# A trunk layer's first modulation: shifts from column groups of the PE array, input scaling and low parts on DVE

## Chip, cores and metric

One core of one Trainium2 chip runs the whole layer. The metric is the device time of one execution in microseconds; three executions of the kernel before took 1581.88, 1586.55 and 1586.59 us (median 1586.55).

## What is computed

A hybrid trunk layer on 1024 latent and 256 context tokens with 1024 features: RMS norm and modulation, a wide input projection, two recurrent mixers (mLSTM and HGRN2), an output projection, a second norm and modulation, a convolutional feed-forward part and a last norm. The part that this document is about is its beginning:

```python
mod_l = (jax.nn.silu(c) @ w_mod[l] + b_mod[l])[:, None, :]
mod_c = (jax.nn.silu(c_ctx) @ w_mod[l] + b_mod[l])[None, None, :]
sh1, sc1, g1, sh2, sc2, g2 = jnp.split(mod_l, N_MOD, axis=-1)
sh1c, sc1c, g1c, sh2c, sc2c, g2c = jnp.split(mod_c, N_MOD, axis=-1)
pl = _modulate(_rmsnorm(xl, norm1_w[l]), sh1, sc1) @ w_in[l]
pc = _modulate(_rmsnorm(xc, norm1_w[l]), sh1c, sc1c) @ w_in[l]
# _modulate(h, shift, scale) = h * (1 + scale) + shift
```

## The kernel before, in words

Everything is float32. A matmul on the fast path takes a pair: `hh` is x rounded to the matmul's format, `hl` the remainder, and the weights likewise `wh` and `wl`; the product is hh·wh + hh·wl + hl·wh. Features lie on the partitions, in eight blocks of 128 (k = 0 to 7), tokens along the free dimension.

**Loading and norm.** SP's queue loads small tensors, then the eight blocks of x (L197), then, in the order of the string `LOADS`, shift weights (`sh_load`, L236), scale weights (`sc_load`, L244) and value weights (`w_load`). ACT squares the blocks, DVE sums them, TensorE adds over the partitions (`row_rstd`, L216), POOL takes the power -1/2, and `row_bc` (L226) spreads the result over all partitions into `rbc`, in two halves.

**First modulation.** j = 0 is the conditioning vector c (latent tokens), j = 1 is c_ctx (context). The scale columns come from DVE dot products with an accumulator: `mod_scale(k, j)` (L260) multiplies block k of the transposed weights with silu(c), broadcast over the partitions in `scb[j]`, and sums along the row. The shift columns come in two ways: for k in `MPE` = (1, 5) from eight matmuls with two moving columns (`mod_shift_mm`, L248; each float32 matmul is two instructions in the trace), for the other six k from a second DVE dot product inside `mod_scale`, once for j = 0 and once for j = 1.

**h.** For k = 0 (`DN`), DVE's `h_scale` (L279) forms x·rbc·a in one operation, ACT adds the shift and rounds (`h_hi`), and DVE forms the remainder (`h_lo`). For the others POOL multiplies x by rbc (`h_norm`, L275), ACT forms hh with scale and shift and then the unrounded value over x (two operations, L288 and L289), and DVE subtracts (L299).

**Rounds.** The value projection of the mLSTM goes in three rounds of token groups: LAT0 (the loop at L400; five token tiles in five PSUM banks, 3 x 5 matmuls a step), LAT1 (L437, three tiles) and CTX (L471, two tiles), with the gate matmuls (L459) between. `split` casts half a weight tile on ACT (`wh`) and subtracts on DVE or POOL (`wl`), two halves a call. In the loop of LAT0 the split of every second k goes to POOL (L405). In the loop of LAT1 the scales and shifts of j = 1 are formed (`mod_scale(order[k], 1)`, L447), and after steps 4 and 7 four context blocks each go through POOL (norm), ACT and DVE (`h_ctx`, L431). From L454 and L476 on, DVE also does the first dot products of the second modulation (`mod2_tile`).

**Order.** In this whole part the order of the instructions on ACT, SP, DVE, POOL and TensorE is the order in the source (`manual_schedule`, L80 and L175); every engine works its queue in that order. After L492 ACT and TensorE keep a hand-written order and a planner orders DVE, POOL and SP. Small PSUM tiles (`sc_tile`) rotate over three banks.

Of the kernel before, what the change touches and what calls it, by code (L numbers as in the profile page):

```python
# [35 lines left out]
QF = (0, 1, 2)  # L36
MPE = (1, 5)
DN = (0,)
MODR = (2, 4, 5, 6, 6, 6, 6, 6, 6)
# [38 lines left out]
def kernel(ctx: ExitStack, tc: tile.TileContext, A: dict, out: bass.AP):  # L78
# [102 lines left out]
    SY.dma_start(out=crow, in_=A["crow"])  # L181
    scc = sp.tile([P, 16], F32, name="scc")
    S.activation(scc, cc, AF.Silu)
    scb = [vp.tile([P, D], F32, name="scl"), sp.tile([P, D], F32, name="scb")]
# [46 lines left out]

    sccv = scc.rearrange("p (j k) -> p k j", k=KD)
    modw = {}
    modc = [(sp2.tile([P, 2], F32, name="sh", bufs=8), sp2.tile([P, 2], F32, name="a1", bufs=8)) for _ in range(KD)]

    def sh_load(k):  # L236
        if k in MPE:
            modw["h", k] = sp2.tile([P, KD, P], F32, name="wsh", tag="ld", bufs=8)
            SY.dma_start(out=modw["h", k], in_=A["wsh"][k].rearrange("p (a c) -> p a c", a=KD))
        else:  # L240
            modw["h", k] = sp2.tile([P, D], F32, name="wsh", tag="ld", bufs=8)
            SY.dma_start(out=modw["h", k], in_=A["wsc"][k * P:(k + 1) * P, :])

# [3 lines left out]

    def mod_shift_mm(k):  # L248
        modw["m", k] = sc_tile("md")
        for kk in range(KD):  # L250
            PE.matmul(modw["m", k][:, 0:2], modw["h", k][:, kk, :], sccv[:, kk, :], start=(kk == 0), stop=(kk == KD - 1))

    def mod_shift_out(k):
        V.tensor_scalar(modc[k][0], modw["m", k][:, 0:2], bmod[:, k:k + 1], None, op0=ALU.add)

    def mod_dot(w, j, dst):
        junk = w if j else stage("junk", 2)
        V.scalar_tensor_tensor(junk, w, 1.0, scb[j], op0=ALU.mult, op1=ALU.mult, accum_out=dst)

    def mod_scale(k, j):  # L260
        aj = modc[k][1][:, j:j + 1]
        mod_dot(modw["c", k], j, aj)
        if k not in MPE:
            hj = modc[k][0][:, j:j + 1]
            mod_dot(modw["h", k], j, hj)
            V.tensor_scalar(hj, hj, bmod[:, k:k + 1], None, op0=ALU.add)
        V.tensor_scalar(aj, aj, b1[:, k:k + 1], n1w[:, k:k + 1], op0=ALU.add, op1=ALU.mult)
# [14 lines left out]
    def h_hi(k, j):  # L282
        x_, hi = h_cols(k, j)
        sh, a1 = modc[k]
        if j == 0 and k in DN:
            S.activation(hi, x_, AF.Identity, bias=sh[:, 0:1])
            return
        S.activation(hi, x_, AF.Identity, bias=sh[:, j:j + 1], scale=a1[:, j:j + 1])  # L288
        S.activation(x_, x_, AF.Identity, bias=sh[:, j:j + 1], scale=a1[:, j:j + 1])  # L289

    def h_lo(k, j):
# [3 lines left out]
        lo = hl[k][:, 0:TC] if j else hl[k][:, TC:TA]  # L295
        if j == 0 and k in DN:
            V.scalar_tensor_tensor(lo, x_, modc[k][0][:, 0:1], raw(hi), op0=ALU.add, op1=ALU.subtract)
        else:
            V.tensor_tensor(lo, x_, raw(hi), op=ALU.subtract)  # L299
# [34 lines left out]

    def v_mm(po, toks, k, wh, wl, mid=None, ks=(0, KD - 1)):
        for x, w, first, last in ((hh, wh, True, False), (hh, wl, False, False), (hl, wh, False, True)):
            if last and mid is not None:
                mid()
            for t in toks:
                PE.matmul(po[t], x[k][:, t * P:(t + 1) * P], w, start=(k == ks[0] and first), stop=(k == ks[1] and last))  # L340
# [30 lines left out]
    load("w", 2)  # L371
    mod_scale(0, 0)
    wgr = sp.tile([P, KD, 16], F32, name="wgr")
    wgt = sp.tile([P, KD, 32], F32R, name="wgt")
    rbc = stage("rbc", 1)
    row_bc(rrs[0], 4, rbc[:, x7g[0]])
    h_scale(0, rbc, x7g[0])
    row_bc(rrs[1], 4, rbc[:, x7g[1]])
    h_scale(0, rbc, x7g[1])
    if 1 in MPE:  # L380
        mod_shift_mm(1)
    h_hi(0, 0)
    for k in range(1, 1 + NA):
        if k not in DN:
            h_norm(k, rbc, 0, G)
    mod_scale(1, 0)
    split(V)
    load("w", 3)
    SY.dma_start(out=wgr, in_=A["wgt"].rearrange("p (a c) -> p a c", a=KD))
    if 1 in MPE:  # L390
        mod_shift_out(1)
    h_lo(0, 0)
    if 1 in DN:
        h_scale(1, rbc, slice(0, T))
    h_hi(1, 0)
# [4 lines left out]
    for k in range(KD):  # L400
        v_mm(po, LAT0, k, *wq[k], mid=(lambda: mod_shift_mm(2)) if k == 0 and 2 in MPE else None)
        if k + 3 in MPE:
            mod_shift_mm(k + 3)
        if k % 2 == 0:
            split(G)  # L405
        if k + 2 < KD:
            if k + 2 in MPE:
                mod_shift_out(k + 2)
            mod_scale(k + 2, 0)
        if k + 1 < KD:  # L410
            h_lo(k + 1, 0)
        if k + 2 < KD:
            h_hi(k + 2, 0)
        if k in (2, 4, 6):
            load("w", k // 2 - 1)
        if k + 1 + NA < KD:
            h_norm(k + 1 + NA, rbc, 0, G)
        if k == KD - 2:
# [1302 lines left out]
```

## Time and profile before

| what | value |
|---|---|
| median of three runs | 1586.55 us |
| profiled execution | 1585.19 us |
| its span, first to last instruction | 1583.4 us |
| mean granted TensorE clock | 0.977 |
| TensorE busy (matmuls) | 1504.9 us, 95% |
| DVE / ACT / POOL busy | 1136.1 / 551.2 / 639.1 us |
| first hgrn value matmul (L547) | 127.92 us |

The page of the profile gives shares over the whole span; TensorE is busy in 95% of it, and the chain of work that ended last lies on TensorE for 71%. The first tenth of the span looks different from the rest, so the rows below are taken from there: the stretches are cut at the round's first and last matmuls and at the moments at which the granted clock changed. PEclk is the share of full speed that was granted: 1.00 is 2.4 GHz and 0.50 is 1.2 GHz.

### The profile page before, as it was taken

The numbers are of one execution on the slowest core, as the hardware profiler recorded it, in microseconds if no ns is written. First come the engines' busy times: TensorE is split into PE (matmuls) and PEld (weight loads), VectorE is DVE, ScalarE is ACT, GpSimd is POOL, SyncE is SP. The second block draws the span as 40 slices with busy tenths as digits, with TensorE's granted clock in tenths as the row PEclk, the third lists the DMA queues.
The fourth block names the chain that finished last, engine by engine and source line by source line (L and its number), as shares of the span: only waits on it lengthen the run. The fifth ranks groups of instructions, "written<-read, shape, count | busy, mean of one in ns | idle before, by whom it ended". The sixth has DMA issues, their size and how long they took to land.

```text
span 1583.4 us, 22327 instructions
## 1 busy us (share of the span) xinstructions
PE 1504.9 (95%) x8822; PEld 1226.3 (77%) x8822; DVE 1136.1 (72%) x1474; ACT 551.2 (35%) x948; POOL 639.1 (40%) x525
## 2 busy tenths in 40 slices
PE   7889999999899999998999999999999998998998
PEld 4667788888777787877867888888888886886886
DVE  6996666879567776767487989889898898226334
ACT  4543242443232442434463322222222223224332
POOL 3665234453335645443322433333333335335341
PEclk7899999999999999999999999999999999999999
DMA  9235541212032111024667111111111114111112
GB/s 368 88 121 158 171 121 40 67 57 72 32 108 70 42 55 42 30 74 140 218 205 284 54 41 54 53 41 53 52 42 54 43 38 159 54 54 41 43 38 106
DMA packets 47790, 141.76 MB, mean 90 GB/s; under 512 B 4803, under 2 KB 14915, under 8 KB 47686
## 3 DMA queue, kind: packets, MB, share of 16 engines
q1 hardware_dynamic: 47686, 140.34, 26.1%
q8 instruction: 69, 1.13, 0.3%
q14 instruction: 35, 0.29, 0.1%
HBM read 119.81 MB, written 12.13 MB: 83 GB/s over the span
## 4 chain that ended last, share of the span: by engine, by line
PE 71%; DVE 7%; POOL 2%; issue 2%; ACT 2%; DMA 1%; POOLq 0%; SPq 0%; ACTq 0%; DVEq 0%
PE pu L1432 29%; PE pd L1578 14%; PE po L1288 3%; PE pl_hg L512 3%; PE pl_zb L512 3%; PE pl_zf L512 3%; PE pl_mo L512 2%; PE pl_mq L512 2%; PE pc L512 1%; PE pl_hq L512 1%; PE ap L1091 1%; DVE G L1493 1%; POOL QQ L1128 1%; PE st L879 1%; PE pl_mk L512 1%
## 5 line engine op out<-in xcount | busy, mean ns | idle before, releaser
L1432 PE MATMUL pu<-low,wh 128*128 128x512 f32 x1216 | 374.5, 389 | 0.0
L135 ACT CAST wh<-wst 128x512 fp32r<-128x512 f32 x184 | 112.0, 620 | 529.6 <-issue 227.5
L137 POOL TENSOR_TENSOR wl<-wst,wh 128x512 fp32r<-128x512 f32 x114 | 150.7, 1324 | 355.8 <-ACT wh L135 342.7
L1432 PEld LDWEIGHTS pu<-low,wh 128*128 128x128 f32 x1216 | 228.3, 188 | 47.4
L1432 PE MATMUL pu<-low,wl 128*128 128x512 f32 x608 | 236.5, 389 | 0.0
L1493 DVE SCALAR_TENSOR_TENSOR G<-pu,fcw,G 128x945 f32<-128x945 f32 (+2 forms) x168 | 205.3, 1222 | 23.9 <-ACT G L1486 19.0
L1493 DVE SCALAR_TENSOR_TENSOR cb<-pu,fcw,cb 128x945 f32<-128x945 f32 (+2 forms) x168 | 205.3, 1222 | 23.7 <-ACT cb L1486 17.6
L1578 PE MATMUL pd<-wh,gd 128*128 128x512 f32 x624 | 196.7, 397 | 11.7 <-DVE gd L1526 6.9
L1526 DVE TENSOR_TENSOR gd<-G,gd 128x1024 fp32r<-128x1024 f32 x41 | 57.1, 1393 | 131.2 <-ACT gd L1525 131.0
L1578 PEld LDWEIGHTS pd<-wh,gd 128*128 128x128 f32 x624 | 119.6, 192 | 38.3 <-DVE gd L1526 8.0
L1128 POOL TENSOR_TENSOR QQ<-QQ,FF 128x256 f32<-128x256 f32 x112 | 108.1, 987 | 81.5 <-PE ap L1091 41.3
L1432 PEld LDWEIGHTS pu<-low,wl 128*128 128x128 f32 x608 | 114.2, 188 | 23.6
L1578 PE MATMUL pd<-wl,gd 128*128 128x512 f32 x312 | 123.6, 396 | 0.0
L1524 POOL TENSOR_TENSOR wl<-wst,wh 128x512 fp32r<-128x512 f32 x40 | 73.5, 1840 | 115.1 <-ACT wh L1523 115.0
L137 DVE TENSOR_TENSOR wl<-wst,wh 128x512 fp32r<-128x512 f32 x70 | 57.7, 844 | 56.6 <-ACT wh L135 56.4
L1525 ACT CAST gd<-G 128x1024 fp32r<-128x1024 f32 x43 | 45.0, 1049 | 132.8 <-PE pd L1578 126.1
L1578 PEld LDWEIGHTS pd<-wl,gd 128*128 128x128 f32 x312 | 59.8, 192 | 12.7
L331 POOL TENSOR_TENSOR wl<-wst,wh 128x512 fp32r<-128x512 f32 x26 | 50.0, 1943 | 46.3 <-ACT wh L329 26.4
L1121 DVE TENSOR_TENSOR KK<-KK,FF 128x768 f32<-128x768 f32 (+1 forms) x56 | 52.1, 941 | 15.9 <-PE tps L1107 12.5
L1555 POOL TENSOR_TENSOR G<-G,cb 128x1024 f32<-128x1024 f32 x22 | 53.9, 2451 | 14.9 <-DVE cb L1493 14.9
L877 POOL TENSOR_SCALAR kw<-ktok,WS 128x128 f32<-128x128 f32 x60 | 23.9, 399 | 53.7 <-PE st L879 53.5
L1084 ACT COPY X<-KK 128x512 f32<-128x512 f32 x40 | 26.9, 682 | 46.6 <-DVE KK L1121 33.6
(395 smaller groups left out, 3147.7 us busy)
## 6 DMA issues: line engine op xcount, KB each, us to landing
wst<-in_wup_dram SPq DMA_DIRECT2D x44, 512.0 KB, 3.2
wst<-in_wcm_dram SPq DMA_DIRECT2D x28, 512.0 KB, 3.3
wst<-in_wmod_dram SPq DMA_DIRECT2D x26, 512.0 KB, 3.4
wst<-in_wout_dram SPq DMA_DIRECT2D x24, 512.0 KB, 3.5
wst<-in_wdown_dram SPq DMA_DIRECT2D x22, 512.0 KB, 3.2
wst<-in_wvml_dram SPq DMA_DIRECT2D x10, 512.0 KB, 3.5
x<-in_xcT_dram SPq DMA_DIRECT2D x8, 512.0 KB, 6.5
wsc<-in_wsc_dram SPq DMA_DIRECT2D x8, 512.0 KB, 8.8
```

What stands on the lines that cost most here:

```text
L135: S.copy(wh, st[:, hs_])
L137: (eng or G).tensor_tensor(wl, st[:, hs_], raw(wh), op=ALU.subtract)
L331: eng.tensor_tensor(wl, si, raw(wh), op=ALU.subtract)
L512: PE.matmul(o, w[:, ws], x[k][:, c0:c1], start=(k == 0 and pi == 0), stop=(k == KD - 1 and pi == 2))
L1121: V.tensor_tensor(kv, kv, tk, op=ALU.mult)
L1128: G.tensor_tensor(qv, qv, tq, op=ALU.mult)
L1432: PE.matmul(pl[:, gs], w[:, ws], x[k][:, gs], start=(k == 0 and pi == 0), stop=(k == KD - 1 and pi == 2))
L1493: V.scalar_tensor_tensor(a3[:, r0:r1, c0:c1], s3[:, r0 + dy:r1 + dy, c0 + dx:c1 + dx], wcol((dy + 1) * 3 + dx + 1), a3[:, r0:r1, c0:c1], o ...
L1524: G.tensor_tensor(wl, src, raw(wh), op=ALU.subtract)
L1526: (G if dh == 0 and c < 3 else V).tensor_tensor(gl, Gt[c], raw(gh), op=ALU.subtract)
L1555: G.tensor_tensor(Gt[j], Gt[j], cb, op=ALU.mult)
L1578: PE.matmul(po[t], x[:, ts_], w, start=(c == 0 and pi == 0), stop=(c == NF - 1 and pi == 2))
```

## The change

All shift columns come from TensorE now, for both j at once. The silu of both vectors is written into two of 32 zeroed columns per block (`sccp`), so that a block is a 128x32 stationary operand; the shift weights, 128 columns a block and now loaded in the layout of `wsh` for every k, are the moving one. `mod_mm` sends blocks kk and kk + 4 to the column group of 32 that kk names, so four partial sums lie on four groups of 32 partitions; `mod_copy` brings them to SBUF on ACT, `mod_flip` sums and transposes them with a matmul against two selection columns (`sel`, loaded from the start of `lmask0`), and `mod_out` adds the bias on DVE. `mod_scale` keeps its scale dot product only. Every k takes the way of k = 0: `h_scale` on DVE, one ACT operation, and `h_lo` with the shift added. The splits inside the loop of LAT0 go to DVE. `h_norm` on POOL stays for the context blocks only.

```diff
-    scc = sp.tile([P, 16], F32, name="scc")
-    S.activation(scc, cc, AF.Silu)
+    sel = sp.tile([P, 2], F32, name="sel")
+    SY.dma_start(out=sel, in_=A["lmask0"][:, 0:2])
+    sccp = sp.tile([P, KD, 32], F32, name="sccp")
+    V.memset(sccp, 0.0)
+    S.activation(sccp[:, :, 0:2], cc.rearrange("p (j k) -> p k j", k=KD), AF.Silu)
...
-    def mod_shift_mm(k):
-        modw["m", k] = sc_tile("md")
+    def mod_mm(k):
+        modw["p", k] = md = sc_tile("md")
         for kk in range(KD):
-            PE.matmul(modw["m", k][:, 0:2], modw["h", k][:, kk, :], sccv[:, kk, :], start=(kk == 0), stop=(kk == KD - 1))
...
+            j = slice(32 * (kk % 4), 32 * (kk % 4) + 32)
+            PE.matmul(md[j, 0:P], sccp[:, kk, :], modw["h", k][:, kk, :], start=(kk < 4), stop=(kk >= 4))
+
+    def mod_copy(k):
+        modw["s", k] = sp2.tile([P, TC], F32, name="mds", tag="sqc")[:, 0:P]
+        S.copy(modw["s", k], modw["p", k][:, 0:P])
+
+    def mod_flip(k):
+        PE.matmul(modw["p", k][:, P:P + 2], modw["s", k], sel, start=True, stop=True)
+
+    def mod_out(k):
+        V.tensor_scalar(modc[k][0], modw["p", k][:, P:P + 2], bmod[:, k:k + 1], None, op0=ALU.add)
...
-        mod_dot(modw["c", k], j, aj)
-        if k not in MPE:
-            hj = modc[k][0][:, j:j + 1]
-            mod_dot(modw["h", k], j, hj)
-            V.tensor_scalar(hj, hj, bmod[:, k:k + 1], None, op0=ALU.add)
+        w = modw["c", k]
+        V.scalar_tensor_tensor(w if j else stage("junk", 2), w, 1.0, scb[j], op0=ALU.mult, op1=ALU.mult, accum_out=aj)
...
-    mod_scale(0, 0)
...
+    mod_mm(0)
+    mod_copy(0)
     row_bc(rrs[0], 4, rbc[:, x7g[0]])
+    mod_scale(0, 0)
+    mod_flip(0)
+    mod_out(0)
     h_scale(0, rbc, x7g[0])
     row_bc(rrs[1], 4, rbc[:, x7g[1]])
+    mod_mm(1)
+    mod_copy(1)
     h_scale(0, rbc, x7g[1])
-    if 1 in MPE:
-        mod_shift_mm(1)
-    h_hi(0, 0)
-    for k in range(1, 1 + NA):
-        if k not in DN:
-            h_norm(k, rbc, 0, G)
-    mod_scale(1, 0)
+    mod_flip(1)
     split(V)
...
+    h_hi(0, 0)
+    mod_out(1)
     h_lo(0, 0)
-    if 1 in DN:
-        h_scale(1, rbc, slice(0, T))
+    mod_scale(1, 0)
+    h_scale(1, rbc, slice(0, T))
     h_hi(1, 0)
...
     for k in range(KD):
-        v_mm(po, LAT0, k, *wq[k], mid=(lambda: mod_shift_mm(2)) if k == 0 and 2 in MPE else None)
-        if k + 3 in MPE:
-            mod_shift_mm(k + 3)
-        if k % 2 == 0:
-            split(G)
-        if k + 2 < KD:
-            if k + 2 in MPE:
-                mod_shift_out(k + 2)
-            mod_scale(k + 2, 0)
+        n = k + 2
+        v_mm(po, LAT0, k, *wq[k], mid=((lambda: mod_mm(n), lambda: mod_copy(n)), (lambda: mod_flip(n),)) if n < KD else ())
         if k + 1 < KD:
             h_lo(k + 1, 0)
-        if k + 2 < KD:
-            h_hi(k + 2, 0)
+        if n < KD:
+            mod_scale(n, 0)
+            mod_out(n)
+            h_scale(n, rbc, slice(0, T))
+            h_hi(n, 0)
+        if k % 2 == 0:
+            split(V)
         if k in (2, 4, 6):
             load("w", k // 2 - 1)
-        if k + 1 + NA < KD:
-            h_norm(k + 1 + NA, rbc, 0, G)
```

`v_mm` takes two lists of calls as `mid`, one run after its first set of five matmuls and one after its second.

## Rows read from the trace of the kernel before

**Rows 1.** Stretches: us, busy us (and instructions) of each engine, PEclk, DMA share, GB/s.

```profile
17.43:29.45 12.02, 9.61 (x49) 9.15 (x49) 9.31 (x15) 2.88 (x5) 7.69 (x4) 0.56 1.03 420
29.45:39.35 9.90, 8.03 (x18) 5.83 (x19) 9.79 (x14) 4.69 (x6) 5.42 (x4) 0.50 0.96 353
39.35:49.60 10.25, 5.64 (x25) 4.35 (x25) 10.18 (x9) 4.91 (x6) 8.82 (x4) 1.00 0.57 194
49.60:59.80 10.20, 10.20 (x34) 8.66 (x33) 10.09 (x12) 4.13 (x5) 10.20 (x4) 0.50 0.17 51
59.80:75.87 16.07, 15.11 (x64) 11.49 (x62) 13.88 (x18) 9.86 (x14) 7.56 (x5) 1.00 0.10 33
75.87:106.45 30.58, 26.68 (x114) 19.10 (x114) 28.25 (x47) 13.43 (x27) 23.75 (x20) 0.94 0.36 125
106.45:127.92 21.47, 17.06 (x76) 12.71 (x74) 15.48 (x26) 10.16 (x19) 12.23 (x8) 0.84 0.38 127
```

**Rows 2.** Timeline of PE: start, us, instructions, [idle before <-releaser]; waits, round ends.

```profile
36.12 2.33 PE L340 MATMUL pv<-wh,hl 128*128 128x512 f32 x5
...
49.24 2.19 PE L340 MATMUL pv<-wh,hl 128*128 128x512 f32 x5 [4.61 <-DVE hl L299]
...
74.58 1.29 PE L340 MATMUL pv<-wh,hl 128*128 128x512 f32 x5
...
86.70 0.49 PE L229 MATMUL rb<-cst,rr 128*128 128x128 f32 x2 [2.01 <-POOL rr L223]
...
114.95 1.22 PE L340 MATMUL pv<-wh,hh 128*128 128x512 f32 x2 [2.88 <-ACT wh L329]
...
124.60 0.28 PE L463 MATMUL gpc<-hh,wgt 128*32 128x256 f32 x1
...
127.92 0.49 PE L547 MATMUL pv<-wh,hh 128*128 128x512 f32 x1
```

**Rows 3.** Timeline of DVE, one operation beside POOL and one alone.

```profile
42.60 3.30 DVE L258 SCALAR_TENSOR_TENSOR junk<-wsh,scl 128x1024 f32<-128x1024 f32 x1
...
61.32 1.21 DVE L258 SCALAR_TENSOR_TENSOR junk<-wsc,scl 128x1024 f32<-128x1024 f32 x1
```

**Rows 4.** Timeline of SP's queue, the issue ahead of the x loads.

```profile
1.18 0.33 SPq L181 DMA_DIRECT2D crow<-in_crow_dram  x1
```

**Rows 5.** Timeline of PE: row broadcast; later column-grouped matmuls between 512-wide pairs.

```profile
19.84 4.27 PE L229 MATMUL rb<-cst,rr 128*128 128x128 f32 x16 [0.16 <-POOL rr L223]
...
459.65 0.62 PE L512 MATMUL pl_hq<-hh,wl 128*128 128x512 f32 x2
460.21 0.46 PE L1091 MATMUL ap<-QQ,X 128*32 128x32 f32 x32
460.60 0.73 PE L512 MATMUL pl_hq<-hh,wh 128*128 128x512 f32 x2
```

**Rows 6.** Timeline of ACT: h_hi(0), wh casts, last context block, casts behind it.

```profile
27.74 1.15 ACT L286 ACTIVATE hh<-x,sh 128x1024 fp32r<-128x1024 f32 x1 [3.00 <-DVE x L280]
28.79 1.12 ACT L329 CAST wh<-wst 128x512 fp32r<-128x512 f32 x2
...
110.59 0.60 ACT L288 ACTIVATE hh<-xc,sh,a 128x256 fp32r<-128x256 f32 x1 [1.48 <-DVE a L267]
...
114.30 2.16 ACT L329 CAST wh<-wst 128x512 fp32r<-128x512 f32 x4
```

**Rows 7.** Timeline of POOL: two wl, context scalings, six wl, one alone.

```profile
80.21 4.52 POOL L331 TENSOR_TENSOR wl<-wst,wh 128x512 fp32r<-128x512 f32 x2 [3.79 <-ACT wh L329]
...
95.32 8.34 POOL L277 TENSOR_TENSOR xc<-xc,rc 128x256 f32<-128x256 f32 x8
...
115.03 10.96 POOL L331 TENSOR_TENSOR wl<-wst,wh 128x512 fp32r<-128x512 f32 x6 [11.32 <-issue]
...
125.99 1.28 POOL L137 TENSOR_TENSOR wl<-wst,wh 128x512 fp32r<-128x512 f32 x1
```

**Rows 8.** Groups by line and form, DVE: the second pass's shift dots.

```profile
L258 DVE SCALAR_TENSOR_TENSOR wsh<-wsh,scb 128x1024 f32<-128x1024 f32 x6 | 11.1, 1847 | 0.0
```

More of the change, by code (lines that the diff above doesn't have):

```diff
@@ L36 @@
 QF = (0, 1, 2)
-MPE = (1, 5)
-DN = (0,)
 MODR = (2, 4, 5, 6, 6, 6, 6, 6, 6)
@@ L230, in row_bc @@
         S.copy(dst, rb[:, 0:m * P])
-    sccv = scc.rearrange("p (j k) -> p k j", k=KD)
     modw = {}
-    modc = [(sp2.tile([P, 2], F32, name="sh", bufs=8), sp2.tile([P, 2], F32, name="a1", bufs=8)) for _ in range(KD)]
+    sh1 = sp.tile([P, KD, 2], F32, name="sh")
+    sc1 = sp.tile([P, KD, 2], F32, name="a1")
+    modc = [(sh1[:, k, :], sc1[:, k, :]) for k in range(KD)]
     def sh_load(k):
[L237 to L242, printed above, removed]
+        modw["h", k] = sp2.tile([P, KD, P], F32, name="wsh", tag="ld", bufs=8)
+        SY.dma_start(out=modw["h", k], in_=A["wsh"][k].rearrange("p (a c) -> p a c", a=KD))
     def sc_load(k):
@@ L246, in sc_load @@
         SY.dma_start(out=modw["c", k], in_=A["wsc"][D + k * P:D + (k + 1) * P, :])
-    def mod_shift_mm(k):
-        modw["m", k] = sc_tile("md")
+    def mod_mm(k):
+        modw["p", k] = md = sc_tile("md")
         for kk in range(KD):
-            PE.matmul(modw["m", k][:, 0:2], modw["h", k][:, kk, :], sccv[:, kk, :], start=(kk == 0), stop=(kk == KD - 1))
[L253 to L258, printed above, removed]
+            j = slice(32 * (kk % 4), 32 * (kk % 4) + 32)
[7 more added lines that the diff above has]
+        V.tensor_scalar(modc[k][0], modw["p", k][:, P:P + 2], bmod[:, k:k + 1], None, op0=ALU.add)
     def mod_scale(k, j):
         aj = modc[k][1][:, j:j + 1]
-        mod_dot(modw["c", k], j, aj)
-        if k not in MPE:
-            hj = modc[k][0][:, j:j + 1]
-            mod_dot(modw["h", k], j, hj)
-            V.tensor_scalar(hj, hj, bmod[:, k:k + 1], None, op0=ALU.add)
+        w = modw["c", k]
+        V.scalar_tensor_tensor(w if j else stage("junk", 2), w, 1.0, scb[j], op0=ALU.mult, op1=ALU.mult, accum_out=aj)
         V.tensor_scalar(aj, aj, b1[:, k:k + 1], n1w[:, k:k + 1], op0=ALU.add, op1=ALU.mult)
@@ L284, in h_hi @@
         sh, a1 = modc[k]
-        if j == 0 and k in DN:
+        if j == 0:
             S.activation(hi, x_, AF.Identity, bias=sh[:, 0:1])
@@ L295, in h_lo @@
         lo = hl[k][:, 0:TC] if j else hl[k][:, TC:TA]
-        if j == 0 and k in DN:
+        if j == 0:
             V.scalar_tensor_tensor(lo, x_, modc[k][0][:, 0:1], raw(hi), op0=ALU.add, op1=ALU.subtract)
@@ L333, in w_split, with v_mm @@
         return hs_
-    def v_mm(po, toks, k, wh, wl, mid=None, ks=(0, KD - 1)):
+    def v_mm(po, toks, k, wh, wl, mid=(), ks=(0, KD - 1)):
+        mid = iter(mid)
         for x, w, first, last in ((hh, wh, True, False), (hh, wl, False, False), (hl, wh, False, True)):
-            if last and mid is not None:
-                mid()
+            if not first:
+                for f in next(mid, ()):
+                    f()
             for t in toks:
@@ L389 @@
     SY.dma_start(out=wgr, in_=A["wgt"].rearrange("p (a c) -> p a c", a=KD))
-    if 1 in MPE:
-        mod_shift_out(1)
+    h_hi(0, 0)
+    mod_out(1)
     h_lo(0, 0)
-    if 1 in DN:
-        h_scale(1, rbc, slice(0, T))
+    mod_scale(1, 0)
+    h_scale(1, rbc, slice(0, T))
     h_hi(1, 0)
```

## Prediction

> **What bounds the kernel now.** I read the table of stretches first [rows 1]. After 127.9 us the program is the old one, instruction for instruction as far as the source says; the change can only move the moment at which that part begins. So everything below is about 17.4 to 127.9 us, and the question is which wait ends last there. The TensorE rows of that stretch answer it [rows 2]. The first lat round is the loop over k at L400: eight steps of fifteen 128x512 matmuls, from 29.45 to 75.87 us. TensorE is not its limit: at the upper clock level a set of five costs 1.13 us, a step 3.4 us, all eight 27 us, and the round takes 46. The limit is DVE, busy 9.8 of 9.9, 10.2 of 10.3 and 10.1 of 10.2 us in the first three of the four stretches of the round [rows 1], and TensorE waits for its hl (4.61 us before 49.24) [rows 2]. DVE itself is slowed: the same 128x1024 two-input operation takes 1.21 us alone and 3.30 us while POOL scales x [rows 3]. From 75.9 us on three waits stand out: 2.01 us for POOL's reciprocal root before 86.70, 2.88 us for the wh casts before 114.95, and a lower clock after each of them (mean 0.94 and 0.84 in these two stretches) [rows 1, 2].
>
> **Part 1, up to the third set of k=0: about 0.** Before, that set starts at 36.12 [rows 2]. The load of sel is one more issue ahead of the x loads on SP's queue; the neighbouring issue has 0.33 us [rows 4], and ACT's squares start when the first x lands, so I count 0.4 us for everything. mod_mm(0) now stands ahead of row_bc(0) on TensorE. The nearest rows to it are the column-grouped matmuls of a later stage: 16 of them (32 instructions) sit between two 128x512 pairs; the pair at 459.65 should free TensorE at 460.10 and the next pair starts at 460.60, so the group with both its changes of shape costs 0.50 us [rows 5]. mod_mm has 8 matmuls over 128 columns, not 16 over 32: four instructions of 0.107 us in each column group instead of eight of 0.027, hence 0.72 us at the upper level and about 1.2 at the lower one, which TensorE has here (0.56 and 0.50) [rows 1]. The other bound is that the groups don't overlap: sixteen instructions as in the row broadcast, 4.27 us less its pause and tail, 3.4 us [rows 5]. I take 1.2 because the rows at 460 are the same kind of instruction with the same column groups. mod_flip is two instructions, 0.6 us with its start, ahead of row_bc(1). So rbc comes at 24.7 + 0.4 + 1.2 + 0.6 = 26.9 us, h_scale's second half (some 0.7 us, a little over half of 1.21) ends at 27.7, but ACT still has mod_copy(1), which waits for mod_mm(1) until 27.4, and two wh casts in its queue (1.12 us), so h_hi(0) runs 28.8 to 30.0 (1.15 us) [rows 6]. Then on TensorE: set 1 (2.1 us at the lower level), mod_mm(2) 1.2, set 2 2.1, mod_flip(2) 0.6, which puts the third set at 36.0. It was 36.12 [rows 2], where DVE's split and h_lo (beside POOL) were late; now TensorE's own queue is. No gain, no loss.
>
> **Part 2, the rest of the first lat round: about 0.** Removed from DVE: the shift dots of six of the eight k; removed from its neighbour POOL: seven x scalings and the splits of four weight tiles. Added to DVE: h_scale over 1024 columns (1.21 us) for seven k, and two wl per second k. POOL then does nothing here, so DVE runs at its undisturbed durations [rows 3]. What is late next is a closed chain, for h_lo(n) waits for ACT's h_hi(n), which waits for DVE's h_scale(n), right ahead of it. A step without a split: h_lo 1.2 + dot 1.26 + two small ones 0.4 + h_scale 1.2 + ACT 1.15 + two hand-overs 0.1 = 5.3 us. With a split DVE waits also for the first wh cast and then does two wl: 0.56 + 2 x 0.65 (the 1024-wide one halved is 0.61) = 7.1 us. h_lo(0) begins at 30.0, h_lo(1) at 35.2; six steps follow, three of each kind, 37.2 us: h_lo(7) at 72.4. TensorE then has the three sets of k=7 left, 3.4 us: the round ends at 75.9. It ended at 75.87. What POOL's lock gave away, the chain through ACT takes. TensorE needs 3.4 + 0.72 + 0.3 = 4.4 us a step at the upper level and is hidden under 5.3 to 7.1; at the lower level it needs 8.2 and is not (see the rivals). mod_flip(n) waits on TensorE for mod_copy(n), which is queued on ACT behind h_hi(n-1) and its casts; behind the flip stands only the third set, which needs h_lo of the same step anyway.
>
> **Part 3, from 75.9 to 127.9: -5.3 us.** Here only removal is left. The second pass over the scales loses six shift dots, 11.1 us of DVE [rows 8], and six small additions. Four of the six stand ahead of the first context blocks. POOL, between 80.2 and the first context scaling at 95.32, does six wl and a root, 8.7 us of its own at the 1.28 that a wl has alone; a wl beside a dot has 2.26 (4.52 for two) [rows 7], and with one dot in the way of each of five it needs 13.7 and not 15.1: the context blocks start at about 93.9. The first four then go at ACT's pace (two operations of 0.60 us each [rows 6], and the last h_lo) to 100.0. Three dots of 1.45 us with their small ones remain on DVE before the last context block, not three and two shift dots: the last scale column is ready at 104.4, and ACT takes it up at 104.5; it did at 110.59. From there ACT's queue is unchanged, 3.7 us to the wh cast of 114.30 [rows 6]: now 108.3. TensorE would reach that point at 112.1 less some 1.2 us of the wait before 86.70 (POOL comes to the root earlier) and 1.7 us of lower clock behind it, about 109.2; the wait of 2.88 us and the low clock that followed are gone. Next late is POOL: its wl chain (10.96 us for six) [rows 7] goes at 2.26 us apiece beside the second modulation's dots: four of them from 109.2 end at 118.2, TensorE's last sets a microsecond later at 119.3; they ended at 124.60. With the 3.3 us that follow, the old part begins at 122.6, not at 127.92 [rows 2]. Bounds: only the wait of 2.88 is saved, or also all that the two low-clock stretches and the root cost, 8 us. I take 5.3, nearer the middle, since POOL's wl chain caps it.
>
> **Sum.** 0 + 0 - 5.3 on the profiled execution, 1585.19 us (span 1583.4 and 1.8 around it): 1579.9, say 1580. That execution lies 1.4 below the median of the three runs, 1586.55, which themselves spread over 4.7 us.
>
> **A rule against it.** In the stage with column groups 32 instructions start within 0.4 us, far below the sum of their weight loads and streams [rows 5]. The Trainium skill, page "TensorE: Matmul & The Clock Gate", section "Part 3: Packing small matmuls — row/col tiling", says that a weight load overlaps matmuls in flight only when the row group differs; column groups share all rows. By that rule the groups would run one after another, which is the second rival below; the rows at 460 us speak against it. The page "TensorEngine Tiling (Array Packing)", section "Key Properties", adds that a change of tiling mode drains TensorE; the 0.50 us above contains two such changes.
>
> **Rivals.** *Column groups don't overlap* (the change doesn't do what it says). mod_mm is then 3.4 us at the lower level, and two of them stand ahead of h_hi(0): DVE's chain begins 4.4 us later, the round ends at 80.3, and of the gain of 5.3 there is 0.9 left: 1584. For it: the moving side is four times as wide as in the rows at 460. Against: same instruction, same layout.
>
> *The lower clock stays (slower).* In the round before, 20 of 46 us had the lower level, and it came back only after stretches in which TensorE streamed 512-wide sets without a break; through the row broadcast and the narrow md matmuls it stayed low [rows 1]. Now six of the eight steps hold narrow matmuls and a wait at the flip. A step costs 8.2 us at the lower level against DVE's mean of 6.2. If all is low, the round ends at 30 + 6 x 8.2 + 2 x 6.4 = 92, 16 later: 1596. It decides from the point where the round ends 5.3 us late, at 81: with 34 us of work at the upper level and 62 at the lower one, that is some 60% of it at the lower one; at 85% the round ends at 87.8 and the sum is 1592, which I take for this case. Against: while TensorE is the limit it has no breaks, and that is what brought the level back at 39.35 and 59.8 [rows 1].
>
> *The gain of part 3 is capped earlier*, by POOL's casts and wl: only the 2.88 us wait goes, 1582.3, or less.
>
> *More is gained*: the undisturbed DVE brings the third set of k=0 and each h_lo a little earlier, and no low clock occurs after 59.8 (3 us), with 8 in part 3: 1574.
>
> **Chances.** A measurement of this kernel tells 0.3% (4.8 us) from no change. Forecast 0.56 (own range 1577 to 1583: 0.42 faster by over 0.3%, 0.14 within); no overlap 0.12 (0.10 within, 0.02 slower); capped 0.10 (within); low clock 0.14 (slower); more gained 0.08 (faster). Together 0.50 faster, 0.34 within, 0.16 slower. The range for 8 in 10 goes from 1574 to 1588: it takes in the no-overlap case and half-low clocks, and leaves out the worst of the low clock and a little below.
>
> **What would show it.** Right: no POOL row between 27 and 74 us; 128x1024 operations on DVE at 1.2 us throughout; h_lo spaced 5.3 and 7.1 by turns; the first lat round ending within 1.5 us of 75.9; no wsh operation on DVE after it; ACT's last context block near 104.5; the wait before the casts under 1 us; the first L547 matmul near 122.6. Wrong: mod_mm over 1.5 us, a granted clock of 0.5 through most of the round, or the wl chain of the context ending as late as before. The sum also fails if the later part, whose order a planner sets for DVE, POOL and SP, comes out in another order.

## The result, and the profile after

The changed kernel takes 1572.26 us (median of four, 1571.05 to 1574.69) where the kernel before takes 1584.82: a ratio of 0.9924, 95% interval 0.9902 to 0.9947. Its profiled execution has 1571.65 us (span 1569.8, mean granted clock 0.985, where before had 0.977). The direction was forecast, the size was not: 12.6 us by the medians, 13.5 between the two profiled executions, where the sum said 5.3. Line numbers of the later part are three lower than before (L544 is the old L547).

| moment, us of the span | before | forecast | after |
|---|---|---|---|
| third set of k = 0 starts | 36.12 | 36.0 | 34.40 |
| last set of LAT0 ends | 75.87 | 75.9 | 75.08 |
| POOL's first context scaling | 95.32 | 93.9 | 91.29 |
| ACT's last context block | 110.59 | 104.5 | 102.15 |
| wh casts behind it | 114.30 | 108.3 | 105.86 |
| gpc | 124.60 | 119.3 | 116.17 |
| first hgrn matmul | 127.92 | 122.6 | 119.50 |
| end of the span | 1583.4 | 1578.1 | 1569.8 |

Of the 13.5 us, 8.4 are there at the first hgrn matmul; 5.1 come behind it (5.2 by the spans), in a part whose source is the same. Timeline of TensorE in the changed kernel (start, us, instructions, [idle before <-releaser]), the rows that answer to [rows 2], with mod_mm(1) ahead of the round and two waits at the flip inside it:

```profile
25.61 0.64 PE L250 MATMUL md<-wsh,sccp 128*32 128x128 f32 x16
...
34.40 1.40 PE L341 MATMUL pv<-wh,hl 128*128 128x512 f32 x5
...
40.46 0.38 PE L257 MATMUL md<-sel,mds 128*128 128x2 f32 x2 [1.58 <-ACT mds L254]
...
64.99 0.38 PE L257 MATMUL md<-sel,mds 128*128 128x2 f32 x2 [1.58 <-ACT mds L254]
...
73.79 1.29 PE L341 MATMUL pv<-wh,hl 128*128 128x512 f32 x5
...
83.63 0.71 PE L230 MATMUL rb<-cst,rr 128*128 128x128 f32 x4 [0.90 <-POOL rr L224]
...
108.47 0.74 PE L341 MATMUL pv<-wl,hh 128*128 128x512 f32 x2 [0.56 <-POOL wl L330]
...
116.17 0.28 PE L460 MATMUL gpc<-hh,wgt 128*32 128x256 f32 x1
...
119.50 0.50 PE L544 MATMUL pv<-wh,hh 128*128 128x512 f32 x1
```

The wait of 4.61 us for hl and that of 2.88 us for the casts are gone; four waits of 0.56 to 0.58 us for POOL's wl stand in place of the latter. The table of stretches (us; busy us and instructions of PE, PEld, DVE, ACT, POOL; PEclk; DMA share; GB/s) answers to [rows 1]: from the end of the round to the first hgrn matmul the lower clock level does not occur, where before had means of 0.94 and 0.84.

```profile
17.43:28.72 11.29, 8.85 (x68) 7.94 (x68) 6.04 (x17) 3.79 (x7) 3.04 (x2) 0.69 1.02 415
...
36.87:75.81 38.94, 32.28 (x192) 23.00 (x191) 29.32 (x45) 14.52 (x26) 0.19 (x3) 0.91 0.31 106
75.81:101.84 26.03, 25.13 (x113) 17.88 (x113) 19.88 (x35) 13.44 (x27) 19.46 (x16) 1.00 0.43 147
101.84:119.50 17.66, 14.84 (x76) 10.94 (x74) 11.75 (x17) 9.76 (x19) 12.89 (x9) 1.00 0.38 129
```

Timeline of DVE, two steps of LAT0, one with a split and one without. In the round every 128x1024 operation takes 1.22 to 1.28 us, against up to 3.30 in [rows 3], and the idle time in brackets is the closed chain through ACT that the forecast worked out:

```profile
36.76 1.28 DVE L279 SCALAR_TENSOR_TENSOR x<-x,a,rbc 128x1024 f32<-128x1024 f32 x1
39.76 1.29 DVE L330 TENSOR_TENSOR wl<-wst,wh 128x512 fp32r<-128x512 f32 x2 [1.72 <-ACT wh L328]
40.97 1.28 DVE L296 SCALAR_TENSOR_TENSOR hl<-x,sh,hh 128x1024 fp32r<-128x1024 f32 x1
...
46.24 1.28 DVE L296 SCALAR_TENSOR_TENSOR hl<-x,sh,hh 128x1024 fp32r<-128x1024 f32 x1 [1.22 <-ACT hh L285]
```

ACT (h_hi(0), the last context block, the casts behind it) and POOL, the rows that answer to [rows 6, 7]:

```profile
27.52 1.15 ACT L285 ACTIVATE hh<-x,sh 128x1024 fp32r<-128x1024 f32 x1
...
102.15 0.60 ACT L287 ACTIVATE hh<-xc,sh,a 128x256 fp32r<-128x256 f32 x1 [0.21 <-DVE a L266]
...
105.86 2.24 ACT L328 CAST wh<-wst 128x512 fp32r<-128x512 f32 x4
```

```profile
78.35 3.59 POOL L330 TENSOR_TENSOR wl<-wst,wh 128x512 fp32r<-128x512 f32 x2 [6.04 <-ACT wh L328]
...
91.29 6.46 POOL L276 TENSOR_TENSOR xc<-xc,rc 128x256 f32<-128x256 f32 x8
...
106.61 10.97 POOL L330 TENSOR_TENSOR wl<-wst,wh 128x512 fp32r<-128x512 f32 x6 [8.80 <-issue]
```

### The profile page after: what moved, and what is told of

It reads as the page before. It is cut to its first block, busy times and chain, and to the rows that moved or that the text cites. A ratio compares the mean times of both kernels' runs of the same rounds, so it can differ in the third digit from the quotient of the medians.

```text
span 1569.8 us, 22515 instructions
## 1 busy us (share of the span) xinstructions
PE 1498.0 (95%) x8934; PEld 1216.9 (78%) x8934; DVE 1112.2 (71%) x1460; ACT 543.4 (35%) x949; POOL 599.6 (38%) x510
## 3 DMA queue, kind: packets, MB, share of 16 engines
q8 instruction: 70, 1.15, 0.3%
## 4 chain that ended last, share of the span: by engine, by line
PE 70%; DVE 7%; POOL 3%; ACT 3%; issue 2%; DMA 1%; POOLq 0%; SPq 0%; ACTq 0%; DVEq 0%
PE pu L1429 30%; PE pd L1575 13%; PE po L1285 3%; PE pl_hg L509 3%; PE pl_zb L509 3%; PE pl_zf L509 3%; PE pl_mo L509 2%; PE pl_mq L509 2%; PE pc L509 1%; PE pl_hq L509 1%; PE ap L1088 1%; DVE G L1490 1%; POOL QQ L1125 1%; PE st L876 1%; PE pl_mk L509 1%
## 5 line engine op out<-in xcount | busy, mean ns | idle before, releaser
L135 POOL TENSOR_TENSOR wl<-wst,wh 128x512 fp32r<-128x512 f32 x114 | 150.8, 1325 | 356.0 <-ACT wh L133 343.0
L1521 POOL TENSOR_TENSOR wl<-wst,wh 128x512 fp32r<-128x512 f32 x40 | 73.2, 1833 | 113.8 <-ACT wh L1520 113.8
L330 POOL TENSOR_TENSOR wl<-wst,wh 128x512 fp32r<-128x512 f32 x18 | 31.6, 1775 | 30.8 <-ACT wh L328 22.0
## 6 DMA issues: line engine op xcount, KB each, us to landing
wsh<-in_wsh_dram SPq DMA_DIRECT2D x8, 512.0 KB, 10.1
```

The lines of the kernel that those rows point to most:

```text
L135: (eng or G).tensor_tensor(wl, st[:, hs_], raw(wh), op=ALU.subtract)
L1521: G.tensor_tensor(wl, src, raw(wh), op=ALU.subtract)
```

## Experiments

Two questions: which half of the change pays (the shift columns on TensorE, or the move from POOL to DVE), and where the 5 us behind the first hgrn matmul come from.

**Each half alone.** e3 has the column groups, with POOL, ACT and DVE working on h as before:

```diff
...
+        if k % 2 == 0:
+            split(G)
+        if n < KD:
+            mod_scale(n, 0)
+            mod_out(n)
         if k + 1 < KD:
             h_lo(k + 1, 0)
         if n < KD:
-            mod_scale(n, 0)
-            mod_out(n)
-            h_scale(n, rbc, slice(0, T))
             h_hi(n, 0)
-        if k % 2 == 0:
-            split(V)
+        if k + 1 + NA < KD:
+            h_norm(k + 1 + NA, rbc, 0, G)
...
```

(`h_hi` is its two ACT operations again, and `h_lo` the subtraction. The scale dot stands ahead of `h_lo`, as in the kernel before and in e9; the changed kernel has it behind.)

> The changed kernel with only its first half: the shift columns come from the column groups, but for k of 1 to 7 the input scaling is POOL's again, ACT has its two operations and DVE a plain subtraction, and the splits in the loop of LAT0 are POOL's. Theory (the removal of the second-pass dots carries the gain, the move from POOL to DVE nothing): the first hgrn matmul at 119 to 121, the time 1572 to 1575. Rival (the undisturbed DVE carries a part): DVE's 128x1024 operations take 2 to 3.3 us beside POOL, the first lat round ends 3 us or more later than 75.0, time 1576 to 1580.

e9 is the kernel before with the other half:

```diff
-DN = (0,)
+DN = tuple(range(KD))
...
-        if k % 2 == 0:
-            split(G)
...
         if k + 2 < KD:
+            h_scale(k + 2, rbc, slice(0, T))
             h_hi(k + 2, 0)
-        if k + 1 + NA < KD:
-            h_norm(k + 1 + NA, rbc, 0, G)
+        if k % 2 == 0:
+            split(V)
```

> The kernel before with only the second half of the change: every k takes the way of k = 0 (input scaling on DVE, one ACT operation, remainder with the shift on DVE) and the splits in the loop of LAT0 are DVE's; the shift columns stay dot products on DVE. Theory (the move from POOL to DVE alone brings nothing, DVE being the limit): a step costs DVE two dots 2.5, small ones 0.7, scaling 1.2 and remainder 1.2, that is 5.6, and 3.0 more with a split, so h_lo(7) comes near 76 and the round ends near 79.5, three later than before; 1.2 us come back behind it, since DVE's sums of squares and copies are no longer slowed by POOL; the second pass costs what it cost: first hgrn matmul near 130, time 1585 to 1588. Rival (undisturbed DVE operations pay by themselves): round ends at 72 to 75, time 1579 to 1582.

e3 takes 1572.31 us (ratio to before 0.992, 0.9906 to 0.9935), as much as the whole change; e9 takes 1584.52 (0.9998, 0.9983 to 1.0012), as much as before. So the whole gain is had with the column groups alone; e3's first hgrn matmul comes at 120.18. e3 shows why the other half adds nothing in the changed kernel's order, by its TensorE timeline:

```profile
30.77 2.50 PE L341 MATMUL pv<-wh,hh 128*128 128x512 f32 x5 [3.24 <-ACT hh L285]
...
41.11 2.48 PE L341 MATMUL pv<-wh,hl 128*128 128x512 f32 x5
...
55.10 0.65 PE L250 MATMUL md<-wsh,sccp 128*32 128x128 f32 x16
...
59.59 0.65 PE L250 MATMUL md<-wsh,sccp 128*32 128x128 f32 x16
```

DVE beside POOL makes the start late (third set of k = 0 at 41.11, not 34.40). But from 50 us on a step takes 4.4 to 4.5 us (55.10 to 59.59), TensorE's own pace, since POOL's part runs ahead and no chain through ACT closes. The moved version starts 6.7 us earlier and pays 5.3 and 7.0 a step; the last matmul of the round starts at 75.08 in e3 and at 74.69 in the changed kernel. In e9, with the dots kept, DVE stays the limit, in LAT0 and before CTX, though its round ends at 76.5, where 79.5 was expected (timeline of TensorE):

```profile
68.62 2.50 PE L340 MATMUL pv<-wh,hl 128*128 128x512 f32 x5 [2.80 <-DVE hl L297]
...
114.50 1.22 PE L340 MATMUL pv<-wh,hh 128*128 128x512 f32 x2 [4.50 <-ACT wh L329]
```

**The second-pass dots.** e8 puts them back:

```diff
...
         mod_scale(order[k], 1)
+        if order[k] not in (1, 5):
+            w = modw["h", order[k]].rearrange("p a c -> p (a c)")
+            V.scalar_tensor_tensor(w, w, 1.0, scb[1], op0=ALU.mult, op1=ALU.mult, accum_out=dump)
```

> The changed kernel with the six second-pass shift dots put back on DVE, right behind the scale dot of the same block; their result goes nowhere. Everything else, the order of the later part too, is the changed kernel's. Theory (removing these dots is what part 3 gains): the context blocks and the wh casts come later again, the wait of about 2.9 us before the casts and a lower clock behind it return, the first hgrn matmul comes at 125 to 127.5, the time is 1578 to 1580. Rival (the gain of part 3 comes from the earlier, undisturbed start and the clock, not from the dots): first hgrn matmul at 119.5 to 122, 1572 to 1575.

It takes 1577.3 us (0.9946, 0.9925 to 0.9967), and its first hgrn matmul comes at 124.29. Timeline of TensorE in e8:

```profile
84.79 0.71 PE L230 MATMUL rb<-cst,rr 128*128 128x128 f32 x4 [2.10 <-POOL rr L224]
...
111.78 0.73 PE L342 MATMUL pv<-wh,hh 128*128 128x512 f32 x2 [1.59 <-ACT wh L329]
```

From the start of the last LAT0 matmul to the first hgrn matmul, before needs 52.4 us, the changed kernel 44.8 and e8 49.65 (124.29 - 74.64). So the dots are 4.8 of the 7.6 us; with them the wait before the row broadcast is 2.10 us again (0.90 in the changed kernel), and 1.59 of the 2.88 before the casts are back. That is between the two expectations: the removal carries most of part 3, not all.

**Column groups.** e10 sends all eight blocks to one group:

```diff
-            j = slice(32 * (kk % 4), 32 * (kk % 4) + 32)
-            PE.matmul(md[j, 0:P], sccp[:, kk, :], modw["h", k][:, kk, :], start=(kk < 4), stop=(kk >= 4))
+            PE.matmul(md[0:32, 0:P], sccp[:, kk, :], modw["h", k][:, kk, :], start=(kk == 0), stop=(kk == KD - 1))
...
```

(The copy and the flip take 32 partitions there.)

> The changed kernel with all eight shift matmuls of a block in one column group of 32, one accumulation, so that they follow one another; the copy and the flip take 32 partitions. Theory (the four groups overlap): without them mod_mm takes some 3.4 us at the lower clock level and 1.7 at the upper one, not 1.0 and 0.6; two of them stand ahead of hh of k = 0, so the round begins 2.5 to 4 us later, the rest hides under DVE's steps: first hgrn matmul at 121 to 123, time 1575 to 1577. Rival (the groups already run one after another): the same durations of mod_mm, 1570 to 1574.

Timelines of TensorE, mod_mm in the changed kernel (the lower clock level, then the upper one), then in e10 (likewise):

```profile
20.89 1.08 PE L250 MATMUL md<-wsh,sccp 128*32 128x128 f32 x16
...
36.87 0.65 PE L250 MATMUL md<-wsh,sccp 128*32 128x128 f32 x16
```

```profile
20.91 3.62 PE L249 MATMUL md<-wsh,sccp 128*32 128x128 f32 x16
...
40.48 1.94 PE L249 MATMUL md<-wsh,sccp 128*32 128x128 f32 x16
```

The groups overlap: a factor of three. The price on the kernel is small: LAT0 starts at 31.56 and the first hgrn matmul comes at 121.86, 2.4 us later than with groups (3.5 later than in the repeat e7 below). The time is 1574.31 (0.9937, 0.992 to 0.9954), just under the 1575 to 1577 expected; the changed kernel has 1572.26 and, in e7's four executions, 1574.42, so the times don't show a price.

**The order of the later part.** Behind the first hgrn matmul one difference in order stood out. In the changed kernel the second cast of the first mk tile came out ahead of gsc on ACT (it is emitted behind L492 of the kernel before, so ACT's order too is not the source's alone), POOL's low part and SP's next load came earlier in turn, and DVE's dots of the second modulation stood one place earlier. In before, DVE reaches such a dot ahead of its load, with the gate's chain queued behind it, and TensorE waits. Timeline of DVE, then of TensorE, in the kernel before, then of TensorE in the changed one:

```profile
140.32 1.23 DVE L349 SCALAR_TENSOR_TENSOR wst<-wst,scl 128x1024 f32<-128x1024 f32 x1 [2.07 <-DMA wst<-in_wmod_dram]
...
141.47 0.29 DVE L714 COPY gw<-up 128x128 f32<-128x128 f32 x1
```

```profile
143.96 0.49 PE L727 MATMUL mp<-cst,gw 128*128 128x128 f32 x2 [2.22 <-DVE gw L724]
...
157.19 0.49 PE L749 MATMUL gtp<-cst,gw 128*128 128x128 f32 x2 [0.63 <-DVE gw L745]
```

```profile
133.82 0.49 PE L724 MATMUL mp<-cst,gw 128*128 128x128 f32 x2
...
147.21 0.49 PE L746 MATMUL gtp<-cst,gw 128*128 128x128 f32 x2 [1.90 <-DVE gw L742]
```

e1 gives the kernel before the order of after; its edit is below. e2 gives the changed kernel the order of before: there `mk_cast(1)` stands behind the copies of CTX and `mk_low(1)` behind POOL's memsets.

```diff
...
+    mk_cast(0)
+    mk_cast(1)
     gpc = sc_tile("gpc")
...
     vml_pair(4)
+    mk_low(0)
+    mk_low(1)
```

> The kernel before, with one edit: the split of the first mk weight tile is written out ahead of the gate matmul, so that both its casts stand on ACT ahead of gsc, as they do in the changed kernel; the planner then puts the first dots of the second modulation one place earlier in DVE's queue, as in the changed kernel but for one dot. All of the first 128 us is that of before. Theory (the order of the later part is worth what was not forecast): the wait of 2.22 us for gw before the mp matmuls and the 3.4 us at the lower clock behind it go, with part of the wait before the nd matmuls at 405 us: 4 to 5 us from the first hgrn matmul to the end, a time near 1580.5 where before has 1585. Rival (the 5 us come from the moment at which the part begins, through DMA and clock phases): first hgrn matmul near 127.9 and no change, 1585 within 1.5.

> The changed kernel with before's order in its later part: the second cast of the first mk tile is put behind the copies that follow the gate matmul, its low part behind POOL's memsets, and DVE's dots of the second modulation then stand where they stood before (two small operations of the recurrence apart). Theory (order): the first hgrn matmul still comes near 119.5, and from there to the end it takes 4 to 5 us more than in the changed kernel, with a wait of some 2 us for gw before the mp matmuls: 1576 to 1577. Rival (start moment): 1572, no wait before mp.

e1 takes 1579.17 us (0.9967, 0.9953 to 0.9981): 5 us off before. e2 takes 1572.19 (0.9919, 0.9907 to 0.9931): no loss on the changed kernel. One speaks for the order, the other against it. Since e1's profiled execution was its slowest (1585.52), three profiles were taken again:

> The kernel before, unedited, for a second profiled execution: how far do two executions of one kernel differ, and where? Theory (the clock's low stretches scatter): same waits, among them about 2 us for gw before the mp matmuls, low stretches at other places, total within 3 us of 1585. Rival (the low stretches are fixed by the order of work): the same low stretches as in the first one, within 0.5 us of each other at each landmark.

> The kernel of e1 once more, for a second profiled execution, since the first one (1585.5) was the slowest of its eight (median 1579.2). Theory (the order of the later part is worth about 5 us in a typical execution): 1577 to 1581, with first hgrn matmul to first nd in 111 to 112 us as in the changed kernel, not 114 as in before, and no wait of 2.5 us before pl_mk. Rival (nothing is gained in the later part; the gain lies in the first 128 us): first hgrn matmul at 123 to 125.

> The changed kernel, unedited, for a second profiled execution and more times beside its variants: 1570 to 1575 either way. Theory (scatter of the low stretches): first hgrn matmul at 117 to 121, and the low stretches elsewhere than in the first profile. Rival (fixed): the same landmarks within 0.5 us.

The profiled executions took 1584.87, 1580.45 and 1573.42 us (e7's four have a median of 1574.42, 0.9928, 0.99 to 0.9955). Both executions with e1's edit reach the first hgrn matmul late, at 128.79 and 128.58, so its gain does not lie ahead of it. The wait before mp is set by the order: 2.1 to 2.2 us in the four executions with the order of before (both of before, e2 and e9), none with the order of after (0.2 in e11, whose dots are spread otherwise). But most of it only moves: the wait before gtp is 1.9 us with the order of after, 0.6 and 1.3 in the two executions of before. From the first hgrn matmul to pl_mk the two executions of before need 35.05 and 35.19 us, e2 35.26, the two of the changed kernel 34.46 and 35.45. So the order is no cause of 5 us in the changed kernel; why e1 gains 5 in the median stays open.

The repeats show what one pair of profiles can't: the landmarks of one kernel move by more than a microsecond.

| execution | first LAT0 matmul | first hgrn matmul | from there to the end |
|---|---|---|---|
| before, twice | 29.45, 30.64 | 127.92, 129.10 | 1455.5, 1454.0 |
| after, twice | 28.72, 27.54 | 119.50, 118.32 | 1450.3, 1453.3 |

By these means 9.6 of the 12.6 us lie ahead of the first hgrn matmul and 2.9 behind it. Stretches at the lower clock level lie at different places behind it in two executions of one kernel (before: one from 165.7 in the first, none there in the second). In sum they take 31.9 us there in both executions of before, 29.2 and 28.7 in those of after. An estimate: if all work there went at TensorE's pace, half of such time would be lost, so this difference of 2.9 us is worth 1.5 at most, about half of what is to be explained.

The thirteen traces together point to the clock and not to the order: the five executions with 31.9 to 32.7 us at the lower level behind the first hgrn matmul need 1454.0 to 1455.5 us from it to the end, the eight with 25.0 to 29.3 need 1449.4 to 1453.3. e8, with the order of after, is among the five (1454.7); e2, with the order of before, is among the eight (1450.6). The two executions with e1's edit stand one on each side (1454.9 and 1450.1), though both start at nearly the same moment. No edit changed the clock alone, so this goes together with the 2.9 us and is not shown to cause it.

**Two versions that go further.** The closed chain can be opened by order alone. e4 puts the scale dot ahead of `h_lo`, where the kernel before has it, and the split right behind it:

```diff
-        if k + 1 < KD:
-            h_lo(k + 1, 0)
         if n < KD:
             mod_scale(n, 0)
+        if k + 1 < KD:
+            h_lo(k + 1, 0)
+        if k % 2 == 0:
+            split(V)
+        if n < KD:
             mod_out(n)
             h_scale(n, rbc, slice(0, T))
             h_hi(n, 0)
-        if k % 2 == 0:
-            split(V)
```

> The changed kernel with another order inside a step of LAT0: the scale dot of k+2 and the split stand on DVE around h_lo(k+1) so that DVE works while ACT makes hh, where it waited 1.22 us (1.72 with a split) for it. Theory (the closed chain DVE-ACT-DVE sets the step): steps fall from 5.3 and 7.0 to 4.1 and 5.4, TensorE's own 4.4 is next, the round ends 7 to 9 us earlier, at 66 to 68, and the time is 1564 to 1566. Rival (TensorE at the lower clock, or the arrival of weights, sets the step): the round ends near 74 to 75, 1571 to 1573.

It takes 1561.26 us (0.9852, 0.9839 to 0.9865), 11 less than the changed kernel and almost 3 less than the lower end of what was expected. Timeline of DVE in e4: the scale dot fills the 1.15 us of ACT's hh, and DVE no longer waits for it (but in the last step, which has no dot). Then the last set of the round, timeline of TensorE:

```profile
40.78 1.28 DVE L279 SCALAR_TENSOR_TENSOR x<-x,a,rbc 128x1024 f32<-128x1024 f32 x1
41.98 1.22 DVE L265 SCALAR_TENSOR_TENSOR junk<-wsc,scl 128x1024 f32<-128x1024 f32 x1
...
43.43 1.27 DVE L296 SCALAR_TENSOR_TENSOR hl<-x,sh,hh 128x1024 fp32r<-128x1024 f32 x1
44.62 1.28 DVE L330 TENSOR_TENSOR wl<-wst,wh 128x512 fp32r<-128x512 f32 x2
```

```profile
64.94 1.29 PE L341 MATMUL pv<-wh,hl 128*128 128x512 f32 x5
```

Steps fall to 4.0 and 5.2 us, and the last set of the round starts at 64.94, not 73.79. Part of this is the clock: from 33.06 to 66.95 e4 has 1.00 throughout, where the changed kernel's round has two stretches at the lower level. Beside e3 (1572.31), which also has the dot ahead of `h_lo`, e4 shows what the move to DVE is worth once the order lets DVE work on: 11 us, the clock included. That the move brings nothing holds for the order of the changed kernel alone. e11 adds an edit in CTX:

```diff
-MODR = (2, 4, 5, 6, 6, 6, 6, 6, 6)
+MODR = (2, 2, 3, 3, 4, 6, 6, 6, 6)
...
         if i in (1, 3):
-            split(G)
+            split(V)
```

> The kernel of e4 with one more edit: in the loop of CTX the splits go to DVE, and DVE's first dots of the second modulation are spread so that they stand behind them. Theory (POOL's low parts at 2.2 us apiece beside DVE's dots cause the four waits of 0.57 us before the CTX sets): the waits go, a low part takes 0.65 us, the first hgrn matmul comes 2 to 2.5 us earlier than in e4 (110.7), near 108.5, and the time is 1558 to 1560. Rival (the gate's chain or the later part gives it back): first hgrn matmul near 108.5 but the time of e4, 1561.

The four waits go: the CTX sets take 10.9 us (from 90.93 to gpc at 101.81), not the 14.4 of e4, and the first hgrn matmul comes at 105.16. The time is 1559.48 us (0.9842, 0.9826 to 0.9858), 1.8 less than e4 with overlapping intervals: of 5.5 us at the first hgrn matmul (2.0 of them there when LAT0 starts, where nothing differs; 108.5 was expected) about two thirds are gone by the end.

## Why the prediction went wrong, by its steps

*What bounds the kernel.* Right in that DVE set the first round and that its operations went slower beside POOL. (The 1.21 us row of [rows 3] is not quite alone, since POOL starts a subtraction inside it at 61.65; the dot at 66.93, with POOL idle, took 1.21 too.) One reading was too short: the statement that after 127.9 us the change can only move the start. It moved a queue order as well, and the two parts differ by 2.9 us over two executions each. The last lines of the prediction named that risk, but neither the sum nor the range had a term for it.

*Part 1 (forecast 0, measured -1.7; -2.9 over two executions each).* The mis-sized term is mod_mm(1) and what hung on it: taken at the lower clock level, 1.2 us, with mod_copy(1) done at 27.4. The granted clock from 17.43 to 28.72 was 0.69, not 0.56; mod_mm(1) took 0.64, the copy ended at 26.6, and h_hi(0) ran at 27.52, not 28.8. Ahead of it the row broadcast was faster than counted (1.63 us for its second half, 2.08 for its first), since the upper level came back during it: from 25.60 to 28.70 the granted clock was 0.97. In the rows of before the prediction had found the level to come back only behind 512-wide sets; here it came back with none between 17.8 and 28.7. mod_flip, counted at 0.6 us, for which no row stood, kept TensorE for 0.29 (23.77 to 24.06). The factor for the column groups was right.

*Part 2 (forecast 0, measured +0.9 on top of part 1, in both pairs of executions).* Right in the chain: steps of 5.27 and 7.0 us against 5.3 and 7.1, DVE undisturbed, waits of 1.22 and 1.72 us for ACT. From h_lo(0) to h_lo(7) it took 42.1 us, where 42.4 were forecast, and h_lo(7) ended at 72.06. That the round still ended 0.9 later against its third set is TensorE's part: it was at the lower level twice, each time behind a wait of 1.58 us at the flip (a wait of 1.56 us before 52.73 had no such stretch behind it). Stretches of the changed kernel (columns as above):

```profile
42.15:45.56 3.41, 3.41 (x22) 2.09 (x21) 2.84 (x6) 0.50 (x1) 0.00 (x0) 0.50 0.99 337
...
66.04:69.46 3.42, 3.42 (x10) 2.64 (x9) 3.38 (x6) 0.00 (x0) 0.00 (x0) 0.50 0.44 153
```

An estimate: six sets at 1.13 us from 65.24 on end at 72.0, so the last set could have started with the end of h_lo(7) at 72.06 and not at 73.79; the second stretch cost up to 1.7 us. The text had such stretches as a rival, but no term for them in the sum. e4 opens the chain, and the round ends 8.9 us earlier, with the stretches gone as well. What the text treated as given was only an order, and one that the change itself had brought in (the dot behind `h_lo`).

*Part 3 (forecast -5.3, measured -7.6 in both pairs).* The dots carried most of it, as forecast: 5.3 for everything against 4.8 for them by e8. What failed is the moment at which POOL's chain begins: the text kept before's 80.2 and put at nothing what the change does to DVE's queue just behind the round. Before, POOL still slowed DVE's sums of squares, the vml copies came late, and LAT1 waited 1.89 us; undisturbed it waits 0.72 (0.71 in e9, which has only the move to DVE, and 1.10 in e3, where POOL still slows the sums). Timeline of DVE there, before, then after:

```profile
74.15 2.96 DVE L316 TENSOR_TENSOR ssqc<-ssqc,sqc 128x256 f32<-128x256 f32 x3 [0.43 <-ACT sqc L315]
77.02 1.28 DVE L343 COPY vml<-pv 128x512 f32<-128x512 f32 x2
```

```profile
73.18 1.48 DVE L315 TENSOR_TENSOR ssqc<-ssqc,sqc 128x256 f32<-128x256 f32 x3
75.06 1.29 DVE L344 COPY vml<-pv 128x512 f32<-128x512 f32 x2 [0.40 <-ACT vml L344]
```

These 1.2 us and the round's end 0.8 earlier let POOL's chain begin at 78.35, not 80.21; with a faster wl that makes the 2.6 us by which the context blocks beat the forecast. The other 0.5 of the 3.1 us at gpc lie in POOL's last wl: from the first of them to gpc the text counted 10.1 us, and both kernels need 9.6 (115.03 to 124.60, 106.61 to 116.17). So POOL's wl chain did cap the stage, and e11 takes that cap away.

The lower clock was no missing term here: the sum had already taken both low stretches as gone, and in the kernel before they cost nothing. The 9.6 us are the same with the lower level (before) and without it. In e5 the first low stretch came ahead of the row broadcast, the waits were others, and from the last LAT0 matmul to the first hgrn matmul it took the same 52.4 us. Timeline of TensorE in e5, against 2.01 and 2.88 us in [rows 2]:

```profile
87.88 0.71 PE L229 MATMUL rb<-cst,rr 128*128 128x128 f32 x4 [0.43 <-POOL rr L223]
...
116.16 1.22 PE L340 MATMUL pv<-wh,hh 128*128 128x512 f32 x2 [4.49 <-ACT wh L329]
```

What TensorE lost ahead of the casts it would have waited for them in any case.

*The later part (no term in the sum, measured -5.2; -2.9 over two executions each).* The order did change, as the last lines of the prediction feared, but e2 shows that the order is not what the changed kernel gains by. The cause stays open; by the estimate above the lower clock can be up to half of the 2.9 us.

*Rivals.* No overlap: refuted by e10, 1.94 us for mod_mm in one group against 0.65 in four; and its price, 4 us in the text, was 2.4 to 3.5 at the first hgrn matmul and not to be seen in the times. The prediction took from the Trainium skill (page "TensorE: Matmul & The Clock Gate", section "Part 3: Packing small matmuls — row/col tiling") that a weight load overlaps matmuls in flight only where the row group differs, and read from it that column groups would run one after another. That reading went too far: the same section gives three column groups a measured speedup of 2.38, and here, where all groups share the rows, e10's 1.94 against 0.65 us decides against it too. The lower clock staying: did not happen; 36.87 to 75.81 had 0.91, with the two stretches of part 2. Capped earlier: did not happen, part 3 gave 7.6. *More is gained* named much of what came (an earlier third set, almost 8 us in part 3) and stood at 0.08, but not the reasons: the third set was early mostly by the clock and not by DVE, and a low stretch did occur after 59.8. With the part behind the first hgrn matmul the result went below its 1574 too, by less than the kernel's own scatter (1574.42 in e7's four executions). The start of POOL's chain in part 3, the clock in part 1 and the range's silence on the later part are what left 1572 out.

## What to carry to other kernels

Price a removed operation on each queue behind it up to the next wait, not only in its own stage, and ask at which moment the next engine's queue can start. When a wait is set by another engine's chain, time lost ahead of it costs nothing. When work moves to the engine that already sets the pace, look for the chain that it closes: here the move gained 6.7 us at the start and lost them again step by step, and moving the dot and the split to either side of the remainder gave 11 us. Where a planner orders queues, put a term of some microseconds into the range, and take a second profile before a difference of 2 us is called an effect.

## What the runs showed of the chip that was not expected

Sixteen column-grouped float32 instructions of 128 moving columns took about a third of the same number in one group: 1.08 against 3.62 us at the lower clock level, 0.65 against 1.94 at the upper one. Two executions of one kernel differed by 1.2 us at the first LAT0 matmul and by 1.5 and 3 us in the 1450 us behind the first hgrn matmul, with lower clock stretches at different places. A stretch at the lower level cost nothing where another engine's chain set the next wait: before and its repeat, with the stretch behind the row broadcast in one and ahead of it in the other, both needed 52.4 us from the last LAT0 matmul to the first hgrn matmul.
